# Level masks made earlier, and four groups of instructions placed later or elsewhere, in a hybrid decoder step

## The chip, the cores and the metric

One core of one Trainium2 chip runs the whole kernel. The metric is the device time of one execution in microseconds (us); smaller is better. Engines are named as in the profile: PE is the matrix engine, PEld its weight load, DVE the vector engine, ACT the scalar engine, POOL the general-purpose engine and SP the engine that issues nearly all transfers.

## The reference

One layer of a decoder, for a prompt of 1024 tokens behind 16 learned meta tokens, and for 8 samples of 4 new tokens each with paged keys and values of 1024 past tokens. All numbers are float32.

```python
h = rms_norm(x, norm_pre_g)                       # 1040 + 32 tokens, 2048 wide
u = h @ w_in                                      # 7184 columns
sq, sk, sv, sg, gq, gk, gv, gg, ga = split(u)     # 8 stick-breaking heads, 4 gated linear heads
# stick-breaking attention, per head
z = q @ k.T * 128**-0.5 + bias
a = where(mask, exp(log_sigmoid(z) - later_sum(softplus(z))), 0)
o_sb = a @ v
# gated linear attention, per head (key 128, value 256 wide)
log_f = log_sigmoid(ga @ w_alpha + b_alpha) / 16
b = cumsum(log_f)
attn[t, s] = sum_k q[t, k] * k[s, k] * exp(b[t, k] - b[s, k])   # s <= t
o = attn @ v + (q * exp(b)) @ S
S_new = exp(b_last) * S + (k * exp(b_last - b)).T @ v
# both groups
mixed = concat(o_sb * silu(sg), rms_norm(o) * silu(gg))
y = x + rms_norm(mixed @ w_out, norm_post_g)
```

The outputs are y for the prompt and for the samples, the new keys and values, and the new states of the gated linear heads.

## The kernel before, in words

**Arithmetic.** A float32 operand is split into a high and a low part, and each product is three matmuls (lines 292 to 294, 1478 to 1480). For each split ACT makes the high part by a cast and DVE the low part by a subtraction: weights of the input projection in lines 182 and 183, those of the output projection in 1315 and 1316.

**Order.** The program is written out by Python generators. A `Weaver` counts beats; each beat stands for six matmuls of the input projection (`inproj`) or, later, for one step of the output projection, and a generator that yields n goes on n beats later. What is written is then ordered for each engine by a planner that goes by priorities and its own costs: an instruction that it takes to be ready may be pulled ahead of others. `urgent()` lifts the priority of weights and of PSUM evacuations. `spread(ins)` ties an instruction in the planned order behind the last projection matmul written, without a semaphore; `add_manual_dep(..., NOSYNC)` ties it behind a named instruction in the same way. Each engine then runs its own queue strictly in the order planned.

**Stages.** First the inputs are normed and transposed. Then come 8 stick-breaking heads: for each, values, keys and queries are projected (evacuated from three PSUM banks by `ev_v`, `ev_k`, `ev_q`, line 632 on ACT and 633 on DVE for the queries), and while the next head is projected the tiles of `attend_tile` run woven into it. The values are written out by token and read back into staging tiles (`vr`) by `load_v`, which casts them to `V` (line 495 ACT, 496 DVE). POOL masks the diagonal tiles (lines 529, 545). All the while DVE makes the samples' logits from paged keys (`z_feed`, line 393, four products `jk` to a page). Then come 4 gated linear heads: `decay` makes the running sums of the log gates (`cb`) by three chunks of columns, each with a matmul, an evacuation `ny` (line 741), a minimum on DVE (742), Exp and Ln on ACT (743, 744), a maximum (745) and scans (751); `level` uses seven masks `lvl` of 128x128 bytes, one for each halving of a chunk; `chunks` carries the state through the prompt and then updates the 8 sample states (`Sb` loaded by `load_state` into four buffers, outputs `os_` in line 962, updates `sn` in 971). The keys `gk` are evacuated by `place` (lines 680 to 688). Then come the gates and paged values, and last the output projection by a seven-product scheme in which `take` adds up PSUM banks and `done` sums the squares for the last norm.

**Staging.** Nearly all short-lived tiles come from one pool of seven buffers (`stage`, tag `stg`), shared by all stages.

The masks are made by `level_masks` at the start of the gated linear stage, one a beat from beat 13 on, by a memset and four affine selects on POOL (lines 712 to 716) and a cast to bytes on DVE (719).

Of the kernel before, what the change touches and what calls it, by code (L numbers as in the profile page):

```python
# [13 lines left out]
U8 = mybir.dt.uint8  # L14
BF16 = mybir.dt.bfloat16
# [67 lines left out]
def hybrid_step(ctx: ExitStack, tc: tile.TileContext, x_prompt, x_sample, cache_k, cache_v, state_gla,  # L83
# [233 lines left out]
    def low_rank():  # L317
# [13 lines left out]
        for c, (lo, hi) in enumerate(CHUNKS):  # L331
            with urgent():
# [2 lines left out]
                act.copy(g[64:96, lo:hi], ps)  # L335
                vec.tensor_tensor(g[32:64, lo:hi], ps, g[0:32, lo:hi].bitcast(F32), ALU.subtract)

    paged = {}

    def page_dma(dst, cache, b, i, hs):  # L340
# [115 lines left out]
    with tc.tile_pool(name="sp", bufs=1) as sp, tc.tile_pool(name="sps", bufs=1, space=PSUM) as sps:  # L456
# [22 lines left out]
                nc.sync.dma_start(outp[0, 0, 8 * KT:REAL, h, :], sv[:32, 2, :])  # L479
                nc.sync.dma_start(os_[:, h, :], sv[32:64, 2, :])  # L480

        def load_v(h, V):

            for c in range(3):
                st = stage(f"vr{h}_{c}")
                sv = st[:].rearrange("p (a d) -> p a d", d=P)
                nt = 3 if c < 2 else 2
                src = new_v_prompt[0, 0, :, h, :]
                pool.memset(st[0:1, :], 0.0)
                nc.sync.dma_start(sv[1:KT + 1, :nt], src[c * 378:c * 378 + nt * KT].rearrange("(a p) d -> p a d", p=KT))  # L490
                if c == 2:
                    nc.sync.dma_start(sv[1:33, 2, :], src[8 * KT:REAL])
                for rows, i0, n in (((KT + 1, 0, 3),) if c < 2 else ((KT + 1, 0, 2), (33, 2, 1))):
                    vs = slice(3 * c + i0, 3 * c + i0 + n)
                    act.copy(V[0][:rows, vs, :], sv[:rows, i0:i0 + n])
                    vec.tensor_tensor(V[1][:rows, vs, :], sv[:rows, i0:i0 + n], V[0][:rows, vs, :].bitcast(F32), ALU.subtract)
                yield 1

# [69 lines left out]
        D1, D2 = 4, 6  # L568
        ORDER = [(1, j) for j in range(8, -1, -1)] + [(0, j) for j in range(4, -1, -1)]

        def values(h):
            V = [sp.tile([P, 9, P], F32R, tag=f"V{i}", name=f"V{i}_{h}") for i in range(2)]
            W.spawn(load_v(h, V))
            return V

        def sample_q(h, qsm, ks):
# [14 lines left out]
        def head(h):  # L591
            def ev_v(c, ps, lo, hi):
                raw = stage(f"vraw{h}_{c}")
                act.copy(raw[:, :hi - lo], ps)
                W.spawn(tok_out(raw, c, lo, hi, h, new_v_prompt, new_v_sample, f"v{h}"))
            if h:
                inproj(C_SV + h * P, ev_v, 0, f"v{h}", SCHUNKS)
            else:
                for c, (lo, hi) in enumerate(SCHUNKS):
                    with urgent():  # L600
                        ev_v(c, first[c][:, :hi - lo], lo, hi)
            kt = [sp.tile([P, KW], F32R, tag=f"k{i}", name=f"k{i}_{h}") for i in range(2)]
            for t in kt:
                pool.memset(t[:, 0:8 * P].rearrange("p (j x) -> p j x", x=P)[:, :, 0:1].bitcast(F32), 0.0)
                pool.memset(t[:, 8 * P:8 * P + 1].bitcast(F32), 0.0)
            ks = sp.tile([P, NSMP], F32, tag="ks", name=f"ks{h}")

            def split_k(raw, c, lo, hi):
                for i0, n, w in ((0, 3, KT),) if c < 2 else ((0, 2, KT), (2, 1, 32)):
                    d = [t[:, (3 * c + i0) * P:(3 * c + i0 + n) * P] if w == KT else t[:, 8 * P:KW] for t in kt]  # L610
                    d = [t.rearrange("p (a x) -> p a x", a=n)[:, :, 1:w + 1] for t in d]
                    r = raw[:, i0 * KT:i0 * KT + n * w].rearrange("p (a x) -> p a x", a=n)
                    act.copy(d[0], r)
                    vec.tensor_tensor(d[1], r, d[0].bitcast(F32), ALU.subtract)
                if c == 2:
                    act.copy(ks[:], raw[:, REAL - lo:hi - lo])
                return
                yield

            def ev_k(c, ps, lo, hi):  # L620
                raw = stage(f"kraw{h}_{c}")
                act.copy(raw[:, :hi - lo], ps)
                W.spawn(split_k(raw, c, lo, hi))
                W.spawn(tok_out(raw, c, lo, hi, h, new_k_prompt, new_k_sample, f"k{h}"))
            inproj(C_SK + h * P, ev_k, 0, f"k{h}", SCHUNKS)
            qt = [sp.tile([P, SEQ], F32R, tag=f"q{i}", name=f"q{i}_{h}") for i in range(2)]
            qsm = sp.tile([P, NSMP], F32, tag="qsm", name=f"qsm{h}")

            def ev_q(c, ps, lo, hi):
                e = min(hi, REAL)  # L630
                a, b_, n = lo - META, e - META, e - lo
                act.activation(qt[0][:, a:b_], ps[:, :n], AF.Copy, scale=QSCALE)
                vec.scalar_tensor_tensor(qt[1][:, a:b_], ps[:, :n], QSCALE, qt[0][:, a:b_].bitcast(F32), ALU.mult, ALU.subtract)
                if hi > REAL:
                    act.activation(qsm[:], ps[:, n:], AF.Copy, scale=QSCALE)
                    W.spawn(sample_q(h, qsm, ks), 5)
            inproj(C_SQ + h * P, ev_q, META, f"q{h}")
            V = values(h)
            W.spawn(attend(h, qt, kt, V), 2)

        W.spawn(z_feed(lambda n: 2), lasting=True)
        W.spawn(weight_forms(), 10, lasting=True)
        for h in range(HEADS):
            if h == HEADS - 1:
                W.spawn(low_rank_weights(), 58)
            head(h)
# [6 lines left out]
    with tc.tile_pool(name="gp", bufs=1) as gp, tc.tile_pool(name="gps", bufs=1, space=PSUM) as gps:  # L653
# [46 lines left out]
                    op(view(dst, 2 * P, (1, 48)), view(src, 2 * P, (1, 48)))  # L700
                op(view(dst, P, (1, P)), view(src, 2 * P - 1, (-1, P)))

        lvl = {}

        def level_masks():

            yield 12
            for m in (64, 32, 16, 8, 4, 2, 1):
                nb = P // (2 * m)
                a = stage(f"lv{m}")[:, :P]  # L710
                av = a.rearrange("p (n two m) -> p n two m", two=2, m=m)
                pool.memset(a, 1.0)
                for two, k0 in ((1, 0), (0, m)):
                    pool.affine_select(av[:, :, two, :], av[:, :, two, :], [[-2 * m, nb], [0, m]], ALU.is_ge, 0.0,
                                       base=-k0, channel_multiplier=1)
                    pool.affine_select(av[:, :, two, :], av[:, :, two, :], [[2 * m, nb], [0, m]], ALU.is_ge, 0.0,
                                       base=k0 + m - 1, channel_multiplier=-1)
                lvl[m] = gp.tile([P, P], U8, name=f"lvl{m}")
                vec.tensor_copy(lvl[m][:], a)
                yield 1  # L720

        W.spawn(level_masks(), 1)

        def xtile(nm):
            return gp.tile([P, XW], F32, tag="X", bufs=4, name=nm)
# [1 line left out]
        def decay(g, cb):  # L727
# [5 lines left out]
            vec.tensor_tensor(wal[64:96, :], raw[64:96], wal[64:96, :].bitcast(F32), ALU.subtract)  # L733
            for c, (lo, hi) in enumerate(CHUNKS):
                n = hi - lo
                yield 5
                ps = gps.tile([P, 512], F32, tag="P", bufs=2, name=f"al{g}_{c}")
                mm(ps[:, :n], wal[:], ga[0][:, lo:hi], start=True, stop=True)
                ny = stage(f"ny{g}_{c}")[:, :n]
                e = stage(f"e{g}_{c}")[:, :n]  # L740
                act.activation(ny, ps[:, :n], AF.Identity, scale=-1.0, bias=nbal[:, g:g + 1])
                vec.tensor_scalar(e, ny, 30.0, None, ALU.min)
                act.activation(e, e, AF.Exp)
                act.activation(e, e, AF.Ln, bias=1.0)
                vec.tensor_tensor(e, ny, e, ALU.max)
                for i in range(3):
# [166 lines left out]
        def chunks(g, at, qt, gv, pv, res):  # L913
# [42 lines left out]
                        mm(os_[32 * j:32 * j + 32, i, f * P:(f + 1) * P], at[:48, 8, 16 + NT * b:48 + NT * b],  # L956
                           gv[f][:48, 8 * P:9 * P], start=(f == 0 and i == 0), stop=False, skip_group_check=True)
            for b in range(NB):
                if b % 4 == 0:
                    for j in range(4):  # L960
                        n = REAL + NT * (b + j)
                        mm(os_[32 * j:32 * j + 32, b // 4, :], qt[:, n:n + 32], Ss[b + j][:], start=False, stop=True,
                           skip_group_check=True)
                Sb = Ss.pop(b)
                km = stg.tile([96, 384], F32R, tag="stg", name=f"km{g}_{b}")[:, :P]
                vec.tensor_scalar(km, pk[:].bitcast(F32), rmask[:, b:b + 1], None, ALU.mult)
                yield 2
                U = gps.tile([P, DV], F32, tag="U", name=f"Us{g}_{b}")
                mm(U[:], km, pv[:], start=True, stop=True)
                sn = stage(f"sn{g}_{b}")[:, :DV]  # L970
                vec.scalar_tensor_tensor(sn, Sb[:], ebl[:, 9 + b:10 + b], U[:], ALU.mult, ALU.add)
                nc.sync.dma_start(new_state_sample[0, b, g], sn)
                if b + 4 < NB:
                    load_state(b + 4)
# [232 lines left out]
    with ExitStack() as out:  # L1207
# [136 lines left out]
            n = next(at) % 6  # L1344
            return accp.tile([P, 512], F32, tag="acc", name=nm) if n < 3 else ops.tile([P, 512], F32, tag="m", bufs=3, name=nm)

        def done(o, tile_, b, jk):

            w = 512 // len(jk)
            for f, j in enumerate(jk):  # L1350
                act.activation(j, o[:, f * w:(f + 1) * w], AF.Square, accum_out=ssq[:, tile_, 2 * b + f:2 * b + f + 1])  # L1351
            vec.tensor_tensor(o, o, gains[b][:], ALU.mult)

        def take(p, q, t, bk):
# [16 lines left out]
            elif p == 3:  # L1371
                o = sums_[t, 2 + q] = ytile(f"y12_{q}_{t}")
                vec.tensor_tensor(o, bk[:], u, ALU.add)
                done(o, t, 2 + q, [bk[:]])
            elif p == 7:
                o = sums_[4 + t, 2 + q]
                with urgent():
                    vec.tensor_tensor(o, bk[:], o, ALU.add)
                done(o, 4 + t, 2 + q, [stage(f"jk{q}_{t}_{f}")[:, :256] for f in range(2)])
            else:  # L1380
                vec.tensor_tensor(u, bk[:], u, ALU.add)
                done(u, 4 + t, q, [bk[:]])

        def before_last(t):

# [185 lines left out]
```

## Time and profile before

| | |
|---|---|
| time, three runs | 2102.87, 2106.34 (median), 3647.29 us |
| profiled execution | 2099.06 us, span 2097.3 us |
| PE busy | 2053.5 us (98%) |
| DVE busy | 1561.0 us (74%) |
| ACT busy | 962.4 us (46%) |
| POOL busy | 81.2 us (4%) |
| granted clock of PE, mean | 0.997 |

The span goes from the first to the last instruction; the profiled execution's time is 1.8 us longer than its span. Busy time is the sum over an engine's instructions. An idle time is put down to the instruction that released the waiting one. The slowest of the three runs stands far off the other two.

### The profile page before, as it was taken

Reading aid. Unit: us, or ns where it says so; the run is one execution under the profiler, and the core shown is the slowest. Engines: PE = TensorE matmul, PEld = TensorE weight load, DVE = VectorE, ACT = ScalarE, POOL = GpSimd, SP = SyncE. Lnnn points to the kernel's source line nnn. Section 1 sums busy time; section 2 is a strip of 40 time slices with the busy share of each in tenths; the row PEclk is TensorE's granted clock in tenths of the full one; section 3 lists DMA queues with packets and bytes.
Section 4 is the critical chain, followed back from the end, with each engine's and each line's share of the span. In section 5 each row is a group of like instructions: output and inputs, shape, how many; then the busy total and the mean of one; then the engine's idle time right before and its main releaser. Section 6 shows DMA issues by size and latency. Waiting matters only on the chain.

```text
span 2097.3 us, 42175 instructions
## 1 busy us (share of the span) xinstructions
PE 2053.5 (98%) x12546; PEld 1865.4 (89%) x12546; DVE 1561.0 (74%) x6372; ACT 962.4 (46%) x2315; POOL 81.2 (4%) x298
## 2 busy tenths in 40 slices
PE   6999999999999999999999999999999999999998
PEld 4999999999999999999899898998988898777776
DVE  7368888889888989898888888887543347453576
ACT  7345555565655556433525335243433325342342
POOL 0000000101000000020000000000000000000000
PEclk9999999999999999999999999999999999999999
DMA  6255554545555442433332433334766675342485
GB/s 203 82 138 153 137 151 136 168 129 152 146 154 141 141 123 77 142 93 78 100 105 78 117 84 101 98 82 140 248 225 229 223 231 190 131 158 73 131 280 187
DMA packets 374912, 301.87 MB, mean 144 GB/s; under 512 B 46489, under 2 KB 315193, under 8 KB 374681
## 3 DMA queue, kind: packets, MB, share of 16 engines
q1 hardware_dynamic: 372488, 298.90, 47.9%
q8 instruction: 99, 1.62, 0.3%
q14 instruction: 133, 1.08, 0.2%
q10 hardware_dynamic: 2192, 0.27, 0.1%
HBM read 241.75 MB, written 57.31 MB: 143 GB/s over the span
## 4 chain that ended last, share of the span: by engine, by line
PE 85%; DVE 7%; DMA 4%; ACT 2%; issue 2%; SPq 0%; DVEq 0%; ACTq 0%; POOL 0%
PE acc_g L292 6%; PE acc_g L293 6%; PE acc_g L294 6%; PE b L1478 4%; PE b L1479 4%; PE b L1480 4%; PE acc_k L292 3%; PE acc_k L293 3%; PE acc_k L294 3%; PE acc_q L292 3%; PE acc_v L292 3%; PE acc_q L293 3%; PE acc_q L294 3%; PE acc_v L294 3%; PE acc_v L293 3%; PE acc_gv L292 2%
## 5 line engine op out<-in xcount | busy, mean ns | idle before, releaser
L393 DVE SCALAR_TENSOR_TENSOR jk<-kp,qb 128x128 f32<-128x128 f32 x2048 | 592.1, 289 | 42.6 <-DMA qb<-qsd 1.7
L292 PE MATMUL acc_g<-hT,wh_g 128*128 128x368 f32 (+2 forms) x768 | 251.2, 327 | 0.0
L293 PE MATMUL acc_g<-hT,wh_g 128*128 128x368 f32 (+2 forms) x768 | 247.2, 322 | 0.0
L294 PE MATMUL acc_g<-hT,wl_g 128*128 128x368 f32 (+2 forms) x768 | 247.0, 322 | 0.0
L1478 PE MATMUL b<-ring,f 128*128 128x512 f32 x416 | 165.3, 399 | 2.7 <-ACT b L1351 1.4
L1316 DVE TENSOR_TENSOR ring<-wr,ring 128x512 fp32r<-128x512 f32 x104 | 70.6, 690 | 129.9 <-ACT ring L1315 129.7
L393 DVE DVE_READ_ACCUMULATOR jk<-kp,qb 128x1 f32 x2048 | 166.3, 81 | 0.0
L1479 PE MATMUL b<-ring,f 128*128 128x512 f32 x416 | 162.6, 391 | 0.7 <-DVE ring L1316 0.7
L1480 PE MATMUL b<-ring,f 128*128 128x512 f32 x416 | 162.2, 390 | 0.0
L292 PEld LDWEIGHTS acc_g<-hT,wh_g 128*128 128x128 f32 x768 | 144.3, 188 | 12.3 <-issue 10.6
L293 PEld LDWEIGHTS acc_g<-hT,wh_g 128*128 128x128 f32 x768 | 144.5, 188 | 0.7
L294 PEld LDWEIGHTS acc_g<-hT,wl_g 128*128 128x128 f32 x768 | 144.3, 188 | 0.8 <-issue 0.8
L1315 ACT CAST ring<-wr 128x512 fp32r<-128x512 f32 x104 | 64.4, 621 | 157.3 <-DMA wr<-in_w_out_dram 74.9
L292 PE MATMUL acc_gv<-hT,wh_gv 128*128 128x384 f32 (+1 forms) x384 | 129.9, 338 | 0.0
L292 PE MATMUL acc_k<-hT,wh_k 128*128 128x378 f32 (+1 forms) x384 | 127.6, 332 | 0.0
L293 PE MATMUL acc_k<-hT,wh_k 128*128 128x378 f32 (+1 forms) x384 | 125.4, 326 | 0.0
L292 PE MATMUL acc_q<-hT,wh_q 128*128 128x368 f32 (+2 forms) x384 | 125.3, 326 | 0.0
L294 PE MATMUL acc_k<-hT,wl_k 128*128 128x378 f32 (+1 forms) x384 | 125.2, 326 | 0.0
L294 PE MATMUL acc_gv<-hT,wl_gv 128*128 128x384 f32 (+1 forms) x384 | 124.6, 325 | 0.0
L293 PE MATMUL acc_gv<-hT,wh_gv 128*128 128x384 f32 (+1 forms) x384 | 124.5, 324 | 0.0
L293 PE MATMUL acc_q<-hT,wh_q 128*128 128x368 f32 (+2 forms) x384 | 123.6, 322 | 0.0
L294 PE MATMUL acc_q<-hT,wl_q 128*128 128x368 f32 (+2 forms) x384 | 123.5, 322 | 0.0
(441 smaller groups left out, 5314.5 us busy)
## 6 DMA issues: line engine op xcount, KB each, us to landing
kp<-in_cache_k_dram SPq DMA_DIRECT2D x512, 64.0 KB
vr<-in_cache_v_dram SPq DMA_DIRECT2D x64, 512.0 KB
tf<-in_w_out_dram SPq DMA_DIRECT2D x64, 256.0 KB
td<-tf SPq DMA_DIRECT2D x64, 256.0 KB
qb<-qsd SPq DMA_DIRECT2D x64, 256.0 KB
wr_g<-in_w_in_dram SPq DMA_DIRECT2D x64, 256.0 KB
wr<-td SPq DMA_DIRECT2D x64, 256.0 KB
wr<-in_w_out_dram SPq DMA_DIRECT2D x48, 256.0 KB
```

The costliest lines, as they stand in the source:

```text
L292: mm(acc[c][:, :n], wh, hh[k][:, lo:hi], start=(k == 0), stop=False)
L293: mm(acc[c][:, :n], wh, hl[k][:, lo:hi], start=False, stop=False)
L294: W.mark = mm(acc[c][:, :n], wl, hh[k][:, lo:hi], start=False, stop=(k == NK - 1)).ins
L393: ins = vec.scalar_tensor_tensor(jk[:], kp[:], 1.0, qbs[h, b][:, t, :], ALU.mult, ALU.mult, accum_out=zt[:, t, NPG - 1 - i:NPG - i])
L1315: act.copy(wh, r)
L1316: vec.tensor_tensor(wl, r, wh.bitcast(F32), ALU.subtract)
L1478: mm(bk[:], ah, wh, start=first and k == 0, stop=False, skip_group_check=True)
L1479: mm(bk[:], ah, wl, start=False, stop=False, skip_group_check=True)
L1480: mm(bk[:], al, wh, start=False, stop=last and k == 7, skip_group_check=True)
```

## The change

1. `level_masks` goes from the gated linear stage to the heads' stage: it is spawned before the first head at a delay of 30 beats and makes a mask every 16 beats. Its results lie in the pool `dk`, which lives through both stages. Its instructions are the same.
2. `load_v` takes the last ACT copy of the head's queries, and each of its casts of V on ACT is tied in the planned order behind that copy.
3. In `decay` the Exp of a chunk is written three beats after the minimum that feeds it, and tied by `spread` behind the last projection matmul written then. A chunk takes 8 beats in place of 6.
4. In `chunks` the products of the second four samples with their old states (`os_`) are written at sample 5 in place of sample 4.
5. In `done` the squares, of which only the sum is used, go to a staging tile in bfloat16 in place of the PSUM bank that the sum came from (products 3 and 4), and for product 7 in one instruction of 512 columns in place of two of 256.

```diff
+    lvl = {}
+    def level_masks():
+        for m in (64, 32, 16, 8, 4, 2, 1):
...
+            lvl[m] = dk.tile([P, P], U8, tag=f"lvl{m}", bufs=1, name=f"lvl{m}")
+            vec.tensor_copy(lvl[m][:], a)
+            yield 16
...
-        def load_v(h, V):
+        def load_v(h, V, behind):
...
-                    act.copy(V[0][:rows, vs, :], sv[:rows, i0:i0 + n])
+                    ins = act.copy(V[0][:rows, vs, :], sv[:rows, i0:i0 + n])
+                    tc.add_manual_dep(ins.ins, behind.name, NOSYNC, reason="behind")
...
-                act.activation(qt[0][:, a:b_], ps[:, :n], AF.Copy, scale=QSCALE)
+                copied.append(act.activation(qt[0][:, a:b_], ps[:, :n], AF.Copy, scale=QSCALE).ins)
...
-            V = values(h)
+            V = values(h, copied[-1])
...
+        W.spawn(level_masks(), 30, lasting=True)
...
-        W.spawn(level_masks(), 1)
...
-                yield 5
+                yield 4
...
                 vec.tensor_scalar(e, ny, 30.0, None, ALU.min)
-                act.activation(e, e, AF.Exp)
+                yield 3
+                spread(act.activation(e, e, AF.Exp))
...
-                if b % 4 == 0:
+                if b in (0, 5):
                     for j in range(4):
-                        n = REAL + NT * (b + j)
-                        mm(os_[32 * j:32 * j + 32, b // 4, :], qt[:, n:n + 32], Ss[b + j][:], start=False, stop=True,
+                        e = b // 5 * 4 + j
+                        n = REAL + NT * e
+                        mm(os_[32 * j:32 * j + 32, b // 5, :], qt[:, n:n + 32], Ss[e][:], start=False, stop=True,
...
-        def done(o, tile_, b, jk):
-            w = 512 // len(jk)
-            for f, j in enumerate(jk):
-                act.activation(j, o[:, f * w:(f + 1) * w], AF.Square, accum_out=ssq[:, tile_, 2 * b + f:2 * b + f + 1])
+        def done(o, tile_, b):
+            jk = stg.tile([P, 512], BF16, tag="stg", name=f"jk{tile_}_{b}")
+            act.activation(jk[:], o, AF.Square, accum_out=ssq[:, tile_, 2 * b:2 * b + 1])
             vec.tensor_tensor(o, o, gains[b][:], ALU.mult)
```

More of the change, by code (lines that the diff above doesn't have):

```diff
@@ L336, in low_rank @@
                 vec.tensor_tensor(g[32:64, lo:hi], ps, g[0:32, lo:hi].bitcast(F32), ALU.subtract)
+    lvl = {}
+    def level_masks():
+        for m in (64, 32, 16, 8, 4, 2, 1):
+            nb = P // (2 * m)
+            a = stage(f"lv{m}")[:, :P]
+            av = a.rearrange("p (n two m) -> p n two m", two=2, m=m)
+            pool.memset(a, 1.0)
+            for two, k0 in ((1, 0), (0, m)):
+                pool.affine_select(av[:, :, two, :], av[:, :, two, :], [[-2 * m, nb], [0, m]], ALU.is_ge, 0.0,
+                                   base=-k0, channel_multiplier=1)
+                pool.affine_select(av[:, :, two, :], av[:, :, two, :], [[2 * m, nb], [0, m]], ALU.is_ge, 0.0,
+                                   base=k0 + m - 1, channel_multiplier=-1)
+            lvl[m] = dk.tile([P, P], U8, tag=f"lvl{m}", bufs=1, name=f"lvl{m}")
+            vec.tensor_copy(lvl[m][:], a)
+            yield 16
     paged = {}
@@ L569, in hybrid_step, with values @@
         ORDER = [(1, j) for j in range(8, -1, -1)] + [(0, j) for j in range(4, -1, -1)]
-        def values(h):
+        def values(h, behind):
             V = [sp.tile([P, 9, P], F32R, tag=f"V{i}", name=f"V{i}_{h}") for i in range(2)]
-            W.spawn(load_v(h, V))
+            W.spawn(load_v(h, V, behind))
             return V
@@ L627, in head @@
             qsm = sp.tile([P, NSMP], F32, tag="qsm", name=f"qsm{h}")
+            copied = []
             def ev_q(c, ps, lo, hi):
@@ L701, in turn @@
                 op(view(dst, P, (1, P)), view(src, 2 * P - 1, (-1, P)))
[L703 to L720, printed above, removed]
-        W.spawn(level_masks(), 1)
         def xtile(nm):
@@ L958, in chunks @@
             for b in range(NB):
[L959 removed]
+                if b in (0, 5):
                     for j in range(4):
[L961 to L962 removed]
+                        e = b // 5 * 4 + j
+                        n = REAL + NT * e
+                        mm(os_[32 * j:32 * j + 32, b // 5, :], qt[:, n:n + 32], Ss[e][:], start=False, stop=True,
                            skip_group_check=True)
[L964 removed]
+                Sb = Ss[b]
                 km = stg.tile([96, 384], F32R, tag="stg", name=f"km{g}_{b}")[:, :P]
@@ L1373, in take @@
                 vec.tensor_tensor(o, bk[:], u, ALU.add)
-                done(o, t, 2 + q, [bk[:]])
+                done(o, t, 2 + q)
             elif p == 7:
@@ L1378, in take @@
                     vec.tensor_tensor(o, bk[:], o, ALU.add)
-                done(o, 4 + t, 2 + q, [stage(f"jk{q}_{t}_{f}")[:, :256] for f in range(2)])
+                done(o, 4 + t, 2 + q)
             else:
                 vec.tensor_tensor(u, bk[:], u, ALU.add)
-                done(u, 4 + t, q, [bk[:]])
+                done(u, 4 + t, q)
         def before_last(t):
```

## The prediction

> **What bounds the kernel now.** I read the page first, then PE's waits over the whole span, then a table of windows of 25 us to see in which stages these waits lie, and last the instructions in order of time around each of them.
>
> ```profile
> span 2097.3 us, 42175 instructions
> PE 2053.5 (98%) x12546; PEld 1865.4 (89%) x12546; DVE 1561.0 (74%) x6372; ACT 962.4 (46%) x2315; POOL 81.2 (4%) x298
> ```
>
> PE sets the time. It is busy in all but 2097.3 - 2053.5 = 43.8 us. The change neither adds nor removes a matmul, so it can win only from these 43.8 us, or from matmuls that run at a lower clock. 2% of the time would be 42 us, nearly the whole of PE's idle time; this is also about what a measurement of this kernel can tell from no change. PE's waits, with the total in us, the times and the longest:
>
> ```profile
> engine line waited for: us in total, times, longest us
> PE tx L262 <- DMA wr_v<-in_w_in_dram: 13.1, 1, 13.1
> ...
> PE acc_v L292 <- DVE q L633: 2.7, 3, 1.5
> PE acc_gq L292 <- ACT gk L681: 2.6, 1, 2.6
> PE b L1478 <- ACT b L1351: 1.4, 2, 0.7
> ...
> PE os L962 <- DMA Sb<-in_state_gla_dram: 1.0, 1, 1.0
> ...
> PE acc_gq L292 <- ACT gk L688: 0.8, 1, 0.8
> PE z L539 <- DVE lo_s L503: 0.8, 2, 0.5
> ```
>
> The last window of the table (us, then PE, PEld, DVE, ACT and POOL busy, PE's clock, share of the transfer engines, GB/s):
>
> ```profile
> 2050.00:2097.30 47.30, 37.29 (x176) 28.05 (x174) 31.47 (x75) 11.95 (x41) 0.00 (x0) 0.92 0.51 179
> ```
>
> The largest wait, 13.1 us for the first weights, is left alone by the change, and so is nearly all of the 47.3 - 37.3 = 10 us at the end, where the last sums are normed and written. Five rows have to do with lines that the change moves: 2.7 + 2.6 + 1.4 + 1.0 + 0.8 = 8.5 us. I take them by the part of the change that meets them.
>
> **Masks and decay's Exp.** This is the passage from the heads' stage to the gated linear stage, with DVE, ACT and PE in order of time (start, duration, instruction, idle time before it):
>
> ```profile
> 901.26 0.51 ACT L741 ACTIVATE ny<-al,nbal 128x304 f32<-128x304 f32 x1
> ...
> 906.86 0.46 ACT L743 ACTIVATE e<-e 128x304 f32<-128x304 f32 x1 [4.90 <-POOL lv L714]
> ...
> 907.96 0.27 ACT L681 COPY gk<-acc_gk 128x128 f32<-128x128 f32 x1
> ```
> ```profile
> 906.47 0.30 DVE L742 TENSOR_SCALAR e<-ny 128x304 f32<-128x304 f32 x1
> ```
> ```profile
> 905.35 0.30 PE L294 MATMUL acc_gk<-hT,wl_gk 128*128 128x304 f32 x1
> 908.28 0.44 PE L292 MATMUL acc_gq<-hT,wh_gq 128*128 128x384 f32 x1 [2.64 <-ACT gk L681]
> ...
> 909.17 0.53 PE L293 MATMUL acc_gq<-hT,wh_gq 128*128 128x384 f32 x1
> ...
> 911.41 0.53 PE L294 MATMUL acc_gq<-hT,wl_gq 128*128 128x384 f32 x1
> 912.78 0.41 PE L292 MATMUL acc_gq<-hT,wh_gq 128*128 128x304 f32 x1 [0.84 <-ACT gk L688]
> ...
> 914.92 0.34 PE L293 MATMUL acc_gq<-hT,wh_gq 128*128 128x384 f32 x1
> 915.09 0.34 PE L294 MATMUL acc_gq<-hT,wl_gq 128*128 128x384 f32 x1
> ```
>
> The third chunk's `ny` is out of ACT at 901.77, but DVE reaches the minimum (L742) only at 906.47, because its queue is full. The row names POOL as what released the Exp; DVE's minimum, which ends at 906.77, is the operand it needed. Exp (L743) stands in ACT's queue ahead of the copies of `gk`, so these begin only at about 907.7, though the last matmul on `gk` ended at 905.65. PE waits for the first bank 2.64 us and again for the third 0.84 us. Between the two, seven matmuls start 2.24 us apart in all (909.17 to 911.41), 0.32 us each; later ones start 0.17 us apart (914.92 to 915.09). That is 7 x 0.15 = 1.05 us more, and about 0.15 for those at its edges: 1.2 us. This place costs 2.64 + 0.84 + 1.2 = 4.7 us.
>
> A row is weighed here against a page. The Trainium skill (TensorE: Matmul & The Clock Gate, the table of practical advice) asks for no idle gap over some 3 us if the clock is to stay up. By that rule the gap of 2.64 us would have cost no clock and the place 3.5 us; the trace shows slow matmuls after 2.64 us, so I count them.
>
> With the Exp written three beats later and behind a later matmul, ACT holds nothing in front of the copies that still waits for DVE. A beat here is six matmuls of 0.17 us, about 1 us. Against the 4.9 us that Exp waited, three beats are not all; but at beats 21 + 3 = 24 the third Exp is tied to the last matmul on `gk`, so that it comes about level with the copies, which are urgent. What may be left is that Exp goes between the copies of the second and the third bank. The table of windows says how full DVE is here (the same columns):
>
> ```profile
> 800.00:875.00 75.00, 75.00 (x455) 72.62 (x454) 69.34 (x320) 44.26 (x96) 6.40 (x27) 1.00 0.39 108
> 895.00:925.00 30.00, 26.52 (x155) 25.77 (x154) 29.15 (x145) 10.43 (x22) 9.54 (x27) 0.94 0.32 86
> ```
>
> DVE is busy 29.15 of 30 us. The masks leave this window with seven DVE casts and the slots that they hold:
>
> ```profile
> L716 POOL TENSOR_SCALAR_AFFINE_SELECT lv<-lv 128x64 f32<-128x64 f32 x14 | 6.0, 447 | 0.1
> L714 POOL TENSOR_SCALAR_AFFINE_SELECT lv<-lv 128x64 f32<-128x64 f32 x14 | 5.2, 394 | 0.1
> L712 POOL MEMSET lv<- 128x128 f32 x7 | 1.4, 204 | 25.1 <-DMA md<-gs 21.9 <-DVE cb L751 1.6 <-DVE e L745 1.1
> ```
> ```profile
> L719 DVE CAST lvl<-lv x7: 215/221/390, 900.2 to 907.7; 128x128 uint8<-128x128 f32 x7
> ```
>
> Seven casts of 0.22 us are 1.5 us of DVE that no longer delay the minimum. Bounds for the place: 0 (another wait at the same spot) and 4.7 us; I take 4.2, nearer the upper end, because both causes of the late Exp are eased. The running sums come at most 6 beats later; they are needed only after the queries' projection, some 24 beats on.
>
> **What the masks cost in the heads' stage.** First a group of POOL's memsets that stand in that stage now, with the idle time before them and what ended it:
>
> ```profile
> L489 POOL MEMSET vr<- 1x384 f32 x24 | 9.4, 409 | 38.5 <-DMA out_dram<-st_v 16.0 <-DVE tf L418 13.9 <-DMA out_dram<-st_k 3.0
> ```
>
> In the new place POOL gets 6.0 + 5.2 + 1.4 = 12.6 us and DVE 1.5 us over some 110 beats. There DVE has 75 - 69.3 = 5.7 us free in 75, and POOL 68.6. Each mask holds one of seven staging buffers for about 12.6 / 7 = 1.8 us. Queued behind it on POOL are the diagonal masks of attention (L529, L545) and the zeroing of `vr`; behind the cast on DVE everything else. The planner sees the cast's operand coming; in the window where the masks are made now, no DVE wait on POOL shows. PE's matmuls on an attention tile come 4 and 6 beats after the data. Bounds: a small gain if attention's order happens to get better (I take none, since the longest idle row of attention is 0.5 us), and 7 x 1.5 = 10.5 us if each mask brought a stall as long as the longest that PE has in this stage (1.5, L633). I take 0.5, near the lower end, since POOL waits for staging slots there already (38.5 us before L489) and PE shows no wait on POOL.
>
> **Casts of V.** Head 1's queries, ACT, DVE and PE:
>
> ```profile
> 215.75 0.60 ACT L495 CAST V<-vr 127x256 fp32r<-127x256 f32 x2 [2.47 <-DMA vr<-out_dram]
> 216.26 0.48 ACT L632 ACTIVATE q<-acc_q 128x384 fp32r<-128x384 f32 x1
> ```
> ```profile
> 217.38 0.44 PE L292 MATMUL acc_v<-hT,wh_v 128*128 128x378 f32 x1 [1.53 <-DVE q L633]
> ```
>
> ACT stands 2.47 us at a cast that waits for its transfer, with the queries' copy behind it, and PE waits 1.53 us for the bank. The other two waits of the row (2.7 in all) are of this kind, in heads 1 and 5; elsewhere the transfer is in time. Behind the last copy of the queries the cast can hold up only attention's own work, some 2 us later, and V is first read by PE about a dozen beats on. If that cover were gone, attention would wait as long as ACT does now, 2.5 us in two heads. Bounds 0 and 2.7; I take 2.5.
>
> **Sample outputs.** SP's issue and PE's wait:
>
> ```profile
> 1435.87 0.47 SPq L921 DMA_DIRECT2D Sb<-in_state_gla_dram  x1
> ```
> ```profile
> 1441.57 0.62 PE L962 MATMUL os<-Sb,gq 128*32 128x256 f32 x2 [0.96 <-DMA Sb<-in_state_gla_dram]
> ```
>
> The last state lands 5.7 us after its issue and PE waits 0.96 us. Two beats more, 2 us or so, are longer than the wait. The buffers of states and queries are held two beats longer; the next head's queries come over 10 beats after that. Bounds 0 and 1.0; I take 0.9.
>
> **Squares.** Between the two rounds of the last pair of products, DVE, ACT and PE:
>
> ```profile
> 2041.19 0.68 DVE L1381 TENSOR_TENSOR u<-b,u 128x512 f32<-128x512 f32 x1
> ```
> ```profile
> 2037.64 0.62 ACT L1315 CAST ring<-wr 128x512 fp32r<-128x512 f32 x1 [2.11 <-DMA wr<-td]
> ...
> 2041.90 0.60 ACT L1351 ACTIVATE b<-u 128x512 f32<-128x512 f32 x1 [1.83 <-DVE u L1381]
> ```
> ```profile
> 2042.68 0.50 PE L1478 MATMUL b<-ring,f 128*128 128x512 f32 x1 [0.73 <-ACT b L1351]
> ```
>
> The sum is out of the bank at 2041.87, and the Square holds the bank until 2042.50. Without it PE could go on about 0.6 us earlier, twice: 1.3 of the 1.4 us, with 0 as the other end. The transfers of weights behind it are set off by PE's progress, so the gain is passed on; I take 1.2. The Trainium skill speaks against this edit: ScalarE: Activation LUTs says that ACT writes PSUM faster than SBUF. Its rows here differ by 0.02 us for 512 columns (0.60 into the bank, 0.62 for a cast into SBUF); by the rule twelve squares would cost 12 x 0.02 = 0.24 us of ACT, off the path. Product 7's pairs of 256 columns become single instructions, which ACT, 46% busy, does not feel.
>
> **The sum.** 4.2 + 2.5 + 0.9 + 1.2 = 8.8 us off, 0.5 on: 8.3 us. Against the profiled execution that is 2099.06 - 8.3 = 2090.8 us. The median shown, 2106.34, and the other run near it, 2102.87, stand 7.3 and 3.8 us above the profiled execution; the middle of these three is 2102.9. From there: 2102.9 - 8.3 = 2094.6, so I forecast **2095 us**, 0.4% less, within 2%.
>
> **The rivals.**
> First: the place at 905 us gets a new wait in the old one's stead, since DVE is full there (29.15 of 30 us) and the low parts of the weights (L183) come from the same queue. Against it: the casts leave, and the sums are not urgent. Then only V, states and squares count: 2.5 + 0.9 + 1.2 - 0.5 = 4.1, so 2099 us.
> Second, slower: POOL's queue. A mask's memset needs a staging slot, which may be released only by a transfer, and attention's selects stand behind it. Such waits are there now: 16.0 + 3.0 us on transfers before the 24 memsets of L489. If seven masks each cost PE over 8.8 / 7 = 1.3 us the change turns out slower. At 2.5 us each, a POOL chain of 1.8 us and 0.7 us of such a wait, it is 17.5 - 8.8 = 8.7 us slower: 2112 us. Against it: the slack of 4 and 6 beats, and no PE wait on POOL today. Beside this stands a rule of the Trainium skill (SBUF — State Buffer, on the port pair that DVE and POOL share): a POOL instruction that reads SBUF and a DVE instruction with two SBUF inputs exclude each other. By it the 28 selects could block DVE for up to 11.2 us in a stage where it is fuller; the trace has DVE without gaps beside the selects, so that it shows no full stop of that length.
> Third: the planned order hardly changes, or the copies are late for a cause other than these; the time stays at 2103 us.
>
> **How the numbers follow.** Forecast 55%, first rival 20%, second 10%, third 10%, the rest 5%, beyond 2% on either side. The lower end of the range is the lowest run, 2099, less all bounds, 4.7 + 2.7 + 1.0 + 1.3 = 9.7, and 3 us for waits that shift: 2086. The upper end takes in the third rival at the highest near run (2106) and the smaller half of the second: 2110. Slower by over 2% needs five times the second rival's price: 3%. Faster by over 2% would need all of PE's idle time: 2%. Within 2%: 95%.
>
> **What would show it.** Right: PE's waits on L681, L688 (in `gk`), L633, `Sb` and L1351 gone or under 0.3 us each, full clock in 895 to 925, PE idle near 35 us, no mask work there. Wrong: PE waiting on `z` (L538, L539) or on L551 near the masks in the heads' stage; on weights' low parts after 905 us; or ACT still ahead of the copies with an Exp.

## The result, and the profile after

| | before | changed | ratio (95% interval) |
|---|---|---|---|
| time, median of 6 runs | 2104.5 us | 2093.7 us | 0.9949 (0.9936 to 0.9962) |
| time, again on another occasion | 2103.8 us | 2092.3 us | 0.9943 (0.9931 to 0.9955) |
| profiled execution, span | 2097.3 us | 2093.3 us | |

The kernel became 0.5% faster, some 11 us; 2095 us had been forecast, 8.3 us less than the reference level taken there. The ratios leave out the one run of 3647 us, without which the first median of before is 2102.9 us. PE's waits in the changed kernel (total in us, times, longest):

```profile
...
PE b L1481 <- DVE u L1384: 1.7, 2, 1.2
...
PE z L558 <- DVE lo_s L522: 1.3, 3, 0.5
PE b L1481 <- ACT gx L468: 1.1, 1, 1.1
PE os L966 <- DMA Sb<-in_state_gla_dram: 1.0, 1, 1.0
PE z L557 <- ACT hi_s L521: 0.9, 2, 0.6
...
PE b L1481 <- ACT u L1363: 0.7, 1, 0.7
...
PE acc_gq L292 <- ACT gk L710: 0.6, 1, 0.6
```

The wait of 2.7 us on the queries' evacuation is gone. That on `gk` has fallen from 3.4 to 0.6 us. That on the Square (1.4) has gone too, but a wait of 1.7 us on DVE's adding up stands in its place, and the wait on `Sb` is as it was, 1.0 us. Windows of the kernel before, and then of the changed one (us, then PE, PEld, DVE, ACT and POOL busy, PE's clock, share of the transfer engines, GB/s):

```profile
205.00:225.00 20.00, 18.19 (x112) 17.02 (x111) 14.96 (x75) 6.94 (x20) 1.25 (x2) 1.00 0.57 154
580.00:600.00 20.00, 19.14 (x119) 18.17 (x117) 16.15 (x80) 7.42 (x20) 1.28 (x3) 1.00 0.53 162
880.00:935.00 55.00, 51.52 (x309) 50.77 (x309) 49.78 (x253) 21.55 (x49) 11.95 (x35) 0.97 0.39 110
```
```profile
205.00:225.00 20.00, 20.00 (x127) 19.44 (x126) 16.85 (x85) 7.90 (x21) 3.57 (x8) 1.00 0.58 164
580.00:600.00 20.00, 20.00 (x127) 19.20 (x126) 16.67 (x80) 7.66 (x23) 1.78 (x3) 1.00 0.59 168
880.00:935.00 55.00, 54.43 (x342) 54.11 (x341) 50.49 (x253) 21.27 (x48) 0.00 (x0) 1.00 0.43 117
```

PE's idle time falls from 1.8 and 0.9 us to nothing where the two heads' casts of V waited, and from 3.5 to 0.6 us, with the clock at 1.00 in place of 0.97, at the passage into the gated linear stage. At the start of the output projection the changed kernel has waits, on `gx` and on a copy `u` (1.1 and 0.7 us), that the profile of before has not.

Over the whole span, though, PE's idle time hardly falls: it was 2097.3 - 2053.5 = 43.8 us, and the page after has

```profile
PE 2050.0 (98%) x12546; PEld 1863.9 (89%) x12546; DVE 1559.3 (74%) x6372; ACT 962.0 (46%) x2299; POOL 82.5 (4%) x298
```

in a span of 2093.3 us, which leaves 43.3 us. In these three windows 5.6 us are gone, but other waits have grown by nearly as much; 1.2 us of that lie in the first 50 us, which the change does not touch. What differs between the two profiles is PE's busy time, 3.5 us less. Some 1.5 us of this is the clock at the passage (half of the 2.96 us that PE is busy at half clock there, shown at the end), and some 1.8 us are products that now run side by side (under Sample outputs). The two profiled executions are also only 3.9 us apart (2099.06 and 2095.12 us), where the medians differ by 11: they do not show the whole gain.

### The profile page after: what moved, and what is told of

It is laid out like the page before. It is cut to its first block, busy times and chain, and to the rows that moved or that the text cites. A ratio compares the mean times of both kernels' runs of the same rounds, so it can differ in the third digit from the quotient of the medians.

```text
span 2093.3 us, 42148 instructions
## 1 busy us (share of the span) xinstructions
PE 2050.0 (98%) x12546; PEld 1863.9 (89%) x12546; DVE 1559.3 (74%) x6372; ACT 962.0 (46%) x2299; POOL 82.5 (4%) x298
## 4 chain that ended last, share of the span: by engine, by line
PE 84%; DVE 8%; DMA 4%; ACT 2%; issue 1%; SPq 0%; POOL 0%; DVEq 0%; ACTq 0%; POOLq 0%
PE acc_g L292 5%; PE acc_g L293 5%; PE acc_g L294 5%; PE b L1481 4%; PE b L1482 4%; PE b L1483 4%; PE acc_k L292 3%; PE acc_k L293 3%; PE acc_k L294 3%; PE acc_q L292 3%; PE acc_q L293 3%; PE acc_q L294 3%; PE acc_v L292 3%; PE acc_v L294 2%; PE acc_v L293 2%; DVE jk L411 2%
```

## The experiments

Six kernels have one or two of the edits, one lacks one, one is the changed kernel again, and four go further. All ratios are to the kernel before, which ran beside them with medians of 2103.4 to 2103.8 us; lines of their profiles are shifted by the lines that they add.

| kernel | median, us | ratio (95% interval) |
|---|---|---|
| edit 1 alone, masks | 2105.1 | 1.0008 (0.9997 to 1.0019) |
| edit 2 alone, casts of V | 2100.3 | 0.9984 (0.9975 to 0.9993) |
| edit 3 alone, decay's Exp | 2104.4 | 1.0004 (0.9993 to 1.0015) |
| edit 4 alone, sample outputs | 2103.1 | 1.0001 (0.9992 to 1.0011) |
| edit 5 alone, squares | 2103.0 | 0.9996 (0.9987 to 1.0004) |
| edits 1 and 3 | 2102.6 | 0.9993 (0.9982 to 1.0004) |
| all but edit 1 | 2095.7 | 0.9962 (0.9949 to 0.9976) |
| all five, again | 2092.3 | 0.9943 (0.9931 to 0.9955) |
| all five, 42 masks | 2108.5 | 1.0027 (1.0016 to 1.0037) |
| all five, product 4's adding up urgent | 2095.4 | 0.9958 (0.9943 to 0.9972) |
| all five, sample products tied | 2091.5 | 0.9938 (0.9924 to 0.9952) |
| all five, both of these and the last gate's Exp | 2091.3 | 0.9940 (0.9925 to 0.9956) |

### The passage at 905 us: two obstacles, one behind the other

Edit 1 alone: 

> The kernel before with edit 1 alone (the masks made in the heads' stage). Theory A (DVE's full queue made the Exp late and the late Exp held the copies; the masks are a small part of that queue): the seven casts of 0.22 us leave the queue, the Exp of the third chunk still stands ahead of the copies and still waits, PE's waits on gk shrink from 3.4 us to 1.5 to 3 us; the time falls by 0.5 to 2 us, to some 2103 us. Theory B (the masks alone made the passage slow): PE's waits on gk go, the clock stays full, and the time falls by 4 to 5 us, to some 2100 us. Theory C (POOL's queue in the heads pays for it): PE waits on z or O grow by several us near the masks and the time is 2105 us or more.

Edit 3 alone: 

> The kernel before with edit 3 alone (decay's Exp three beats later, tied behind a projection matmul). Theory A: the copies of the first two banks of gk no longer stand behind the Exp; PE's waits on gk fall from 3.4 us to under 1 us, the clock stays at 1.00 from 895 to 925 us, and the time falls by 3.5 to 5 us, to some 2100 us. Theory B (the masks alone made the passage slow): DVE stays late, the Exp keeps waiting in front of some copies, and at most 2 us are won, 2102.5 us or more.

Neither won anything that can be measured. The two profiles show why. With the masks gone, ACT still stands at decay's Exp (L742) in front of the copies of the first two banks. The copies of the third stand behind another Exp, that of `level` (L789), which waits for DVE too:

```profile
908.32 0.46 ACT L742 ACTIVATE e<-e 128x304 f32<-128x304 f32 x1 [4.39 <-DVE e L741]
...
912.90 1.06 ACT L789 ACTIVATE X<-X 128x1024 f32<-128x1024 f32 x1 [2.77 <-DVE X L788]
```
```profile
909.74 0.44 PE L292 MATMUL acc_gq<-hT,wh_gq 128*128 128x384 f32 x1 [1.30 <-ACT gk L700]
914.43 0.41 PE L292 MATMUL acc_gq<-hT,wh_gq 128*128 128x304 f32 x1 [2.34 <-ACT gk L707]
```

The kernel before has the same two. The prediction did not show the second; it stands in front of the copies on which PE waited 0.84 us:

```profile
911.25 1.06 ACT L790 ACTIVATE X<-X 128x1024 f32<-128x1024 f32 x1 [2.57 <-DVE X L789]
```

With the Exp written later and the masks still there, the first copies come in time, but DVE stands at the masks' casts until POOL has made them, and the low part of the weights behind these is late:

```profile
904.56 0.37 ACT L680 COPY gk<-acc_gk 128x256 f32<-128x256 f32 x1 [0.34 <-PE acc_gk L294]
```
```profile
903.99 0.66 DVE L719 CAST lvl<-lv 128x128 uint8<-128x128 f32 x1 [1.11 <-POOL lv L716]
...
905.93 0.23 DVE L719 CAST lvl<-lv 128x128 uint8<-128x128 f32 x1 [1.28 <-POOL lv L716]
...
908.46 0.69 DVE L183 TENSOR_TENSOR wl_gq<-wr_gq,wh_gq 128x512 fp32r<-128x512 f32 x1
```
```profile
909.20 0.45 PE L294 MATMUL acc_gq<-hT,wl_gq 128*128 128x384 f32 x1 [2.46 <-DVE wl_gq L183]
```

The third bank's copies then stand behind decay's Exp, and PE waits 1.40 us for them:

```profile
912.01 0.46 ACT L744 ACTIVATE e<-e 128x304 f32<-128x304 f32 x1 [5.88 <-DVE e L742]
```

So theory A of both was wrong for the time: it had the Exp as the cause, and the masks as a small part of DVE's queue. Edit 3 alone comes nearer to its theory B. Edit 1 alone has the time of its theory C, 2105 us, but not its mechanism: PE's waits on `z` are 1.7 us, 0.4 more than before. Either edit alone leaves PE some 3.6 to 3.9 us of waits at the passage, under other names. The same shows when the masks alone are put back:

> The changed kernel with edit 1 taken back (the masks again at the start of the gated linear stage, where they were). Theory A (the Exp's place is what counts): 0 to 2 us slower than the changed kernel, some 2095 us, PE's waits on gk 0.5 to 1.5 us. Theory B (the masks count): 3 to 5 us slower, some 2098 us, with waits on gk over 2 us.

```profile
PE acc_gq L294 <- DVE wl_gq L183: 1.9, 1, 1.9
PE acc_gq L292 <- ACT gk L691: 1.7, 1, 1.7
```

That is 2095.7 us, 3.4 us over all five (2092.3), with 3.6 us of waits at this place, the low parts' among them. It is theory B's time, though the intervals of the two ratios overlap, so that the 3.4 us is not clear of noise. This led to both edits together:

> The kernel before with edits 1 and 3 together (masks earlier and decay's Exp later), which alone changed nothing that can be measured. Theory D (two obstacles one behind the other: with the masks gone the Exp still stands before the copies, with the Exp gone DVE is still too full for the low parts of the weights; only both clear the passage): PE's idle time from 880 to 935 us falls from 3.5 us to under 1 us, the clock there is 1.00, and the time falls by 4 to 7 us, to some 2098 us. Theory E (what the whole change wins beyond its parts comes from somewhere else, the cast of V or the squares together with one of these): less than 2.5 us, 2101 us or more.

The window 880 to 935 us with both:

```profile
880.00:935.00 55.00, 54.26 (x338) 53.94 (x338) 49.76 (x255) 22.09 (x49) 0.00 (x0) 1.00 0.42 115
```

In the trace theory D holds: the idle time is 0.7 us in place of 3.5 to 3.9, and the clock is full. In the time it does not: 0.9993, 1.5 us with an interval from 3.8 us less to 0.8 more, where 4 to 7 us had been expected; by the time it is theory E. The product of what edit 2, edits 1 and 3, edit 4 and edit 5 give is 0.9984 x 0.9993 x 1.0001 x 0.9996 = 0.9974, some 5.5 us; all five give 0.9943 to 0.9949, 11 to 12 us. The whole is worth some 6 us more than these parts. If the half-widths of the five intervals are added as squares, as for independent errors, they make some 5 us (an estimate), so the 6 us are hardly clear of noise. Most of them do not need edit 1: all but edit 1 gives 0.9962, 8.0 us, and the product of edits 2, 3, 4 and 5 is 0.9985, 3.2 us. The traces show 1.8 us of them, under Sample outputs; the rest is not settled.

### Casts of V

> The kernel before with edit 2 alone (casts of V behind the last copy of the queries). Theory A: PE's waits on the queries' evacuation (L633, 2.7 us) go, no wait on O comes in their place, and the time falls by 2 to 3.5 us, to some 2101.5 us. Theory B (the casts now hold up attention instead): waits on z or O grow by 1 to 2.5 us and the time falls by less than 1 us.

The heads' two windows with edit 2 alone:

```profile
205.00:225.00 20.00, 20.00 (x127) 19.20 (x126) 16.53 (x83) 7.42 (x21) 1.95 (x3) 1.00 0.62 167
225.00:580.00 355.00, 355.00 (x2151) 339.94 (x2150) 316.86 (x1435) 204.41 (x481) 30.49 (x106) 1.00 0.53 148
580.00:600.00 20.00, 20.00 (x127) 19.20 (x126) 16.87 (x83) 8.06 (x25) 2.27 (x4) 1.00 0.54 160
```

Theory A holds: no idle time is left, and none comes between. 0.9984 is 3.4 us (1.5 to 5.3), against 2.5 forecast.

### Sample outputs

> The kernel before with edit 4 alone (products of the second four samples written one sample later). Theory A (the planner pulls these products ahead to where it takes the state to have landed, wherever they are written): PE's wait on Sb stays at 0.8 to 1.2 us in the last head and the time within 1 us of before, some 2104.5 us. Theory B (as predicted): the wait goes and the time falls by 0.9 us.

Theory A, for the product that waits: in the last head the planner puts it where it has it in the kernel before, behind the seventh update of a state, and the wait stands:

```profile
1443.19 0.62 PE L963 MATMUL os<-Sb,gq 128*32 128x256 f32 x2 [0.99 <-DMA Sb<-in_state_gla_dram]
```

Of the other three only the first has moved, from behind the second update to behind the third, and PE waits for none of them. I then tied all four behind a projection matmul:

```diff
-                if b in (0, 5):
+                if b in (0, 6):
...
+                        if b:
+                            spread(o_)
```

> The changed kernel with the products of the second four samples written at sample 6 and tied behind the last projection matmul written, so that the planner can't pull them ahead. Theory A (the planner had undone edit 4): PE's wait on Sb, 0.9 to 1.2 us, falls below 0.3 us, and the time falls by 0.5 to 1 us, to some 2092.3 us. Rival (another wait takes its place): the same idle time from 1400 to 1460 us, 0.9 us, under another name.

Some of the products now stand later in PE's order, but the one that waits still follows the seventh update, and its wait is no shorter:

```profile
1432.47 0.62 PE L966 MATMUL os<-Sb,gq 128*32 128x256 f32 x2 [1.26 <-DMA Sb<-in_state_gla_dram]
```

Why the tie does not hold this one later is not shown, and whether PE would stop elsewhere if it really came later is left open.

Edit 4 pays all the same, in another place. The products of four samples write different strips of 32 partitions of one tile. One alone keeps PE busy for 0.62 us; four written one after another, as those of the first four samples are, take 0.64 us together. In the first three heads the kernel before runs the second four one at a time, with matmuls of the projection between them; in the changed kernel two of the four stand side by side. The first four and a single product before (two records to a product), and then a pair after:

```profile
1032.92 0.64 PE L962 MATMUL os<-Sb,gq 128*32 128x256 f32 x8
...
1044.77 0.62 PE L962 MATMUL os<-Sb,gq 128*32 128x256 f32 x2
```
```profile
1039.13 0.63 PE L966 MATMUL os<-Sb,gq 128*32 128x256 f32 x4
```

PE's busy time on `os` over the three heads, before and after:

```profile
935.00:1410.00 475.00, 13.55 (x144) 1.00 0.36 94
```
```profile
935.00:1410.00 475.00, 11.72 (x144) 1.00 0.37 95
```

That is 1.8 us less of PE. It is 13.55 us with edit 4 alone and with edits 1 and 3, 11.72 us with all but edit 1, and 9.88 us with the tied products, of which three stand side by side. So edit 4 gives this only beside other edits that shift the planned order. It was not planned, and the prediction has no term for it. The time of the tied kernel, 2091.5 us, can't be told from that of all five.

### Squares

> The kernel before with edit 5 alone (squares into a staging tile). Theory A (DVE is late at the same place, so that the bank comes no earlier): PE's waits on L1351, 1.4 us, turn into waits on the adding up by DVE in the same place, PE's idle time from 2000 us to the end changes by less than 0.5 us, and the time stays within 1 us of before, some 2104 us. Theory B (as predicted): the waits go with nothing in their place, 1.2 us less, some 2103.3 us.

Theory A, on one row:

```profile
PE b L1477 <- DVE u L1380: 1.9, 2, 1.3
```

The waits on the Square (two, 1.4 us in all) are now two waits on the adding up, 1.9 us in all, at the same stage. DVE is not free to add: low parts and finished rows (L1316, L1427) come first.

```profile
2040.22 0.74 DVE L1427 SCALAR_TENSOR_TENSOR y<-y,r_y,xr 128x512 f32<-128x512 f32 x1
2040.88 0.68 DVE L1380 TENSOR_TENSOR u<-b,u 128x512 f32<-128x512 f32 x1
2041.58 1.29 DVE L1316 TENSOR_TENSOR ring<-wr,ring 128x512 fp32r<-128x512 f32 x2
```

The ratio, 0.9996, can't tell 0 from the 1.2 us forecast; the row can. So I made the adding up urgent in the changed kernel:

```diff
-                vec.tensor_tensor(u, bk[:], u, ALU.add)
+                with urgent():
+                    vec.tensor_tensor(u, bk[:], u, ALU.add)
                 done(u, 4 + t, q)
```

> The changed kernel with the adding up of product 4 made urgent, as that of products 5 and 7 is. Theory A (the bank is late because DVE does other work first): PE's waits on that adding up, 1.7 to 2.3 us, fall below 0.7 us and the time falls by 1 to 2 us, to some 2091.5 us. Rival (the low parts of the weights that DVE then makes later stop PE in turn): waits on the ring grow by as much, and the time stays at 2093.

PE's waits from 2020 to 2050 us, without the edit (all five, again) and with it:

```profile
PE b L1481 <- DVE u L1384: 2.3, 1, 2.3
```
```profile
PE b L1483 <- DVE ring L1320: 0.7, 2, 0.5
PE b L1482 <- ACT ring L1319: 0.5, 1, 0.5
```

Half of the wait comes back as waits on the weights' two parts. The time, 2095.4 us, is not better than that of all five (2092.3 and 2093.7): theory A's mechanism is there, its gain is not.

### The price of a mask in the heads' stage

```diff
-        for m in (64, 32, 16, 8, 4, 2, 1):
+        for m in (64, 32, 16, 8, 4, 2, 1) * 6:
...
-            yield 16
+            yield 8
```

> The changed kernel with every mask made six times over in the heads' stage, 42 in place of 7 and one every 8 beats. The prediction's bounds for one mask there were 0 and 1.5 us, with 0.07 us taken. Theory A (covered by the slack of attention): 35 more masks cost 0 to 3 us, some 2095 us. Theory C (the slower rival, POOL's queue): each costs PE 1 us or more, so 35 us or more, some 2130 us, with PE waiting on z near them.

35 more masks cost 2108.5 - 2092.3 = 16.2 us, 0.46 us each (medians of two occasions): neither theory's number, but far from free. PE's waits on attention's tiles, and the longest of them traced back, PE and then POOL:

```profile
PE z L557 <- ACT hi_s L521: 8.6, 6, 3.5
PE z L558 <- DVE lo_s L522: 2.6, 8, 0.5
```
```profile
298.07 0.45 PE L557 MATMUL z<-hi_s,ntri 127*127 127x402 f32 x1 [3.46 <-ACT hi_s L521]
```
```profile
291.47 0.20 POOL L346 MEMSET lv<- 128x128 f32 x1 [2.15 <-DMA out_dram<-st_k]
...
296.86 0.28 POOL L564 TENSOR_SCALAR_AFFINE_SELECT Y<-Y 127x126 f32<-127x126 f32 x1
```

The slower rival's mechanism is there: a mask's memset waits 2.15 us for a staging slot that a transfer holds, attention's select comes only behind the masks' selects, ACT waits 4.35 us for it, and PE stops for 3.46 us. PE's waits on `z` are 11.2 us here, 2.2 us with seven masks and 1.3 us before. With seven masks it costs PE 0.9 us (0.5 us in the second profile). At 0.46 us each they would cost 3.2 us; whether seven masks spaced twice as far cost as much apiece, no run shows.

### The changed kernel once more

> The changed kernel once more, for the spread from profile to profile. Its profile showed 3.2 us of waits of PE from 1460 to 2000 us (on the last gate's copy, on a copy in the output projection, on weights) that the kernel before has not. If they are chance (transfers that land a little later), they are smaller here and the profiled time is some 2 us below the first one's 2095.1; if the change's order makes them, they come again within 0.3 us each. The time is 2093.7 within 2 us either way.

The time is the same (2092.3 us), and the waits between 1460 and 2000 us come again, these two within 0.2 us (1.1 and 0.7 us in the profile after):

```profile
PE b L1481 <- ACT gx L468: 0.9, 1, 0.9
...
PE b L1481 <- ACT u L1363: 0.8, 1, 0.8
```

So they are not chance in one execution of the changed kernel. But they don't need all five edits either: the profiles of the kernels with one edit each have a wait of 0.5 to 1.1 us on the copy `gx` too, where the one profile of before has none. How much of the 3 us the kernel before pays in its median can't be read from one profile of it.

### All of it, and the last gate

In the last gate group ACT again runs two Exps ahead of the third copy `gx` (the wait of 1.1 us at L468). This kernel has the two variants above and ties that Exp too:

```diff
-            W.spawn(gate_rest(g, lo, hi, x), 1)
+            W.spawn(gate_rest(g, lo, hi, x), 3 if g == 15 else 1)
...
+        if g == 15:
+            tc.add_manual_dep(ins.ins, evacs[-1].name, NOSYNC, reason="behind")
```

> The changed kernel with both of these (product 4's adding up urgent, the sample products tied) and, in the last gate group alone, the Exp of the gates written two beats later and tied behind the last copy of the group, so that no Exp stands before a copy there. If the three places are independent: PE's waits on the adding up (2 us), Sb (0.9 us) and the last gate's copy (0.9 us) go, 3 to 3.5 us less than the changed kernel, some 2089.5 us. If new waits come in their place: 2092 us or more.

From 1735 to 1800 us that copy's wait is gone, and the wait on the output projection's own copies has grown from 0.7 to 1.9 us:

```profile
PE b L1486 <- ACT u L1367: 1.9, 2, 1.0
```

The wait on `Sb` stays at 1.0 us. At 2091.3 us and 0.9940 (0.9925 to 0.9956) the kernel can't be told from all five. None of these variants is shown to beat the changed kernel.

## Why the prediction was right, point by point

- **What bounds the kernel, and the size of the change.** Right in that PE sets the time and that the gain is a few us. Of the five rows that had been added up, 2.7 us are gone, 2.6 + 0.8 have become 0.6, and the other two (1.4 and 1.0) are not won. Wrong in where the gain must come from: PE's idle time was to fall to 35 us and is 43.3 us in the profile after, and 1.8 us came from matmuls that run side by side, which are neither idle time nor a fuller clock. And 2% is not what a measurement can tell here: with six runs each the interval is 0.13% either way.
- **Masks and Exp, 4.2 us taken.** Right for the two together, by the trace: 2.9 us of idle time and the clock's dip gone. What was left is what had been named, an Exp between the second and the third bank's copies (0.6 us). The reading of the 0.84 us was incomplete: in the kernel before, the Exp in front of the third bank's copies is that of `level`, not decay's. In time the pair alone has not been shown to win anything (1.5 us, from 3.8 less to 0.8 more). The step that said that both causes were eased was right in a way that had not been seen: neither edit is shown to be worth anything alone. And "no DVE wait on POOL shows" was true only of that one schedule; with the Exp alone moved, DVE waits 1.1 and 1.3 us on POOL. The first rival's mechanism, late low parts of the weights, is just what edit 3 alone meets.
- **Masks in the heads' stage, 0.5 us taken.** Right in kind, and about in size by the profiles: 0.9 and 0.5 us more on `z`. The second rival's mechanism exists, at a price per mask below the 1.3 us from which it decides.
- **Casts of V, 2.5 us.** Right; 3.4 us (1.5 to 5.3) measured.
- **Sample outputs, 0.9 us.** Wrong, though small: 0. The step that failed is "two beats more are longer than the wait". What the program writes later, the planner need not place later; the edit left the product that waits where it was. This was the third rival's way, for one product. That edit 4 saves 1.8 us by bringing products together is luck.
- **Squares, 1.2 us.** Wrong in its mechanism: the bank did come free of the Square, but the adding up before it is late in the same place. The step that failed took the adding up's time from the kernel before and held it fixed; with the edit DVE's planned order is another, with a finished row (L1427) ahead of the adding up. The Trainium skill's warning (ScalarE: Activation LUTs, Step-by-step: what each stage is for, on ACT writing PSUM faster than SBUF) was not what decided. In the traces a Square takes 0.60 us into the bank and some 0.63 us into the staging tile, and no wait of PE on a Square is left.
- **The sum.** 8.3 us forecast, some 11 measured, with two terms (2.1 us) gone. That the sum came near the time is in part luck: the products side by side stand for most of these two terms. It was made from a profiled execution of 2099.06 us, near the low end of the kernel before (2098.5 to 2109.0 in 29 runs), and the waits in it were small ones: edit 4 alone moves only products that come later than these waits, and its profiled execution of 2103.7 us has these rows:

```profile
PE acc_v L292 <- DVE q L633: 3.0, 3, 1.6
PE acc_gq L292 <- ACT gk L681: 2.1, 1, 2.1
PE acc_gq L292 <- ACT gk L688: 2.1, 1, 2.1
```

  Here the queries' wait is 3.0 where 2.7 was counted, and that on `gk` 4.2 where 3.4 was. This may account for a part of the difference. Another part is the clock: the mean of the granted clocks on record is 0.9971 in 72 runs of the kernel before and 0.9985 in the 12 runs of the changed one, and 0.0014 of 2100 us is 2.9 us at most (an estimate; the clock is recorded to 0.001), where 1.2 us had been counted. What is left of the 6 us that the parts do not add up to stays open.

## What to carry to other kernels

A wait at a full passage can have two causes in a row, and each then looks worthless when it is tried alone: before an edit is dropped because it did nothing, look which wait took the old one's place. Where a planner orders the queues, an edit that only writes something later may change nothing; look at the order that comes out, at the place where the wait is, and at the others, where it may win or lose something that nobody planned. And when several small waits are to be added up, take them from more than one profiled execution, since the one at hand may be a lucky one.

## What the runs showed of the hardware

PE's clock at the passage did not go by the length of the gap alone. Two waits, of 1.30 and 2.34 us, left it at 1.00 (edit 1 alone); two others, of 2.1 us each, came with 0.97 from 880 to 935 us (edit 4 alone). The stretches at half clock behind these gaps last 3.4 us or twice that. Here is the one of the kernel before, and then, with edit 3 alone, the time ahead of the slow stretch and the stretch itself (us, PE busy, clock, share of the transfer engines, GB/s):

```profile
908.98:912.39 3.41, 2.96 (x10) 0.50 0.07 19
```
```profile
909.00:910.60 1.60, 1.40 (x8) 1.00 0.09 14
910.69:917.51 6.82, 5.42 (x19) 0.50 0.36 96
```

After the gap of 2.46 us with edit 3 alone PE goes on at 909.20 and first runs at full rate for 1.5 us; in the kernel before, the gap of 2.64 us ends at 908.28, and the slow stretch begins 0.7 us later. So what a gap costs in clock is a stretch of this length, or two, or none, and it may begin late; the 1.2 us in the prediction was one draw. What decides which it is, these runs do not show.
